# Layer 1's mixing modulation as row sums on VectorE inside layer 0's feed-forward loop, in place of TensorE products

## The chip, the core and the metric

The kernel runs on one core of a Trainium2 chip. The metric is the device time of one launch in microseconds (us), taken as the median of several runs. A core has TensorE (PE; its weight loads are shown apart as PEld), VectorE (DVE), ScalarE (ACT), GpSimd (POOL) and SyncE (SP). Each engine runs its own instructions in the order in which they stand in its queue and waits on semaphores for the others. Here SP does nothing but issue DMA transfers, also in the order of its queue.

## What is computed

Two layers of a diffusion backbone, for 128 context tokens and 256 latent tokens of width 1024, all in fp32. Each layer is modulated by vectors that come from a condition vector: `c_ctx` for the context, `c` for the latents. Cut to what the change touches:

```python
mod_ctx = (silu(c_ctx) @ w_mod[l] + b_mod[l])[None, :]      # w_mod[l]: 1024 x 6144
mod_lat = silu(c) @ w_mod[l] + b_mod[l]

def layer(x, mod, p, ...):
    sh1, sc1, g1, sh2, sc2, g2 = split(mod, 6)              # 1024 wide each
    h = layer_norm(x) * (1 + sc1) + sh1
    z = h @ p["w_in"] + p["b_in"]                           # q, k, v, conv, fourier, gates
    merged = ga * a_attn + gc * a_conv + gf * a_f           # attention, convolution, Fourier mixing
    x = layer_norm(ALPHA * x + g1 * (merged @ p["w_o"]), ...)
    h = layer_norm(x) * (1 + sc2) + sh2
    u = dwconv(h @ p["w_up"], ...)                          # 1024 -> 5632
    ug, uv = split(u, 2)
    x = layer_norm(ALPHA * x + g2 * ((silu(ug) * uv) @ p["w_down"]), ...)
```

The change concerns `sh1` and `sc1` of layer 1, for both condition vectors: 2 x 1024 sums of 1024 products for each of the two vectors. Layer 1 needs them when its first normalised activations are transposed, at the end of layer 0.

## The kernel before

**Arithmetic.** A matrix product is made of three TensorE products (`mm3`, L192): both operands are split into a high part of type fp32r and a low part that is the rest. For weights, `halves` (L169) does that: ScalarE copies a half of the loaded tile to `whi` (L177), VectorE subtracts it to get `wlo` (L178). There are five buffers for `whi`, five for `wlo` and three for the loaded 1 MB tiles `raw`, so both engines run some tiles ahead of TensorE and are let on as TensorE gives buffers back.

**Order.** The program is written in one order. When it is built, a scheduler places the instructions of each engine in a queue and sets the waits; tiles come from pools with a fixed number of buffers for each tag (`BUFS`, L79), and an instruction that needs a buffer waits for its last user. TensorE's results have two PSUM buffers `ps` and six `acc`. All input loads stand in SP's queue (`load`, L120).

**Modulation.** `setup` (L131) loads the two condition vectors as 16 x 128, takes silu of them (L146 to L148; the result is the tile `ch`), transposes it and keeps it as the stationary operand `cpad`. The modulation is cut into groups A (`sh1`, `sc1`), B (`sh2`, `sc2`) and G (the gates). Group A of layer 0 is made at the start (`mod_first`). All others run through `mod_stream` (L235): a step loads two row blocks of the weights as eight tiles of 256 KB, multiplies them by `cpad` (L215), and adds up in an `acc` buffer over four steps. After the fourth step of an A or B group, `mod_columns` (L276) copies the sums to SBUF (L280, VectorE), turns them into columns with four TensorE transposes (L284) and adds the bias into `modcol` (L292). In layer 0's mixing the stream has three groups, (0,G), (0,B) and (1,A), so twelve steps. `mixing` (L478) calls it once every two tiles of its three branches (L563 to L577). The four steps of (1,A) fall into the last branch.

**Around it.** The last branch makes, for each of eight output tiles, a gate (`ws_tile`, 24 products) and a projection (6 products). VectorE and GpSimd merge them (L531, L532), and the result is split (L535, L536) into `m_hl`. Then come the `w_o` products (`layer`, L814): the first three of the eight row blocks into six `acc` buffers, then the other five for one output part at a time (`tail`), so that closing the first token tile (`close`, L780) overlaps with the products of the next.

**The feed-forward loop** (L902) has 11 rounds. A round makes four tiles of 24 products (`up_tile`, L891) into the two `ps` buffers, each followed by ScalarE's L895 and VectorE's L896 and L898, after which the buffer is free again. VectorE's L914, L916 and L919 and ScalarE's L913 and L918 make the gated result. `down` adds 36 products into `acc`. A round splits six weight halves. The first round's four tiles are made ahead of the loop from unsplit operands (L869), while the three token tiles are closed one after another.

Of the kernel before, what the change touches and what calls it, by code (L numbers as in the profile page):

```python
# [10 lines left out]
F32 = mybir.dt.float32  # L11
F32R = mybir.dt.float32r
AF = mybir.ActivationFunctionType
ALU = mybir.AluOpType
AX = mybir.AxisListType

P = 128
D = 1024
# [59 lines left out]
class Net:  # L78
# [52 lines left out]
    def setup(self):  # L131
        nc, a = self.nc, self.a
        self.zeros = self.const("zeros", [P, P])
        nc.vector.memset(self.zeros, 0.0)
        self.busy(self.WARM)
        self.ident = self.const("ident", [P, P])
        make_identity(nc, self.ident)
        self.mhalf = self.const("mhalf", [P, 1])
        nc.gpsimd.memset(self.mhalf, -0.5)
        self.zero2 = self.const("zero2", [P, 2 * KD])  # L140
        nc.gpsimd.memset(self.zero2, 0.0)
        self.cpad = self.const("cpad", [P, KD, 32])
        nc.gpsimd.memset(self.cpad, 0.0)
        ct, ch = self.kk()[0:2 * KD, :], self.kk()[0:2 * KD, :]
        self.load(ct, a["c2"])
        nc.vector.tensor_scalar(ch, ct, 0.5, None, op0=ALU.mult)  # L146
        nc.scalar.activation(ct, ch, AF.Tanh)
        nc.vector.scalar_tensor_tensor(ch, ct, 1.0, ch, op0=ALU.add, op1=ALU.mult)  # L148
        pt = self.psum()
        nc.tensor.transpose(pt[:, 0:2 * KD], ch, self.ident[0:2 * KD, 0:2 * KD])  # L150
        nc.vector.tensor_copy(
            self.cpad[:, :, 0:2], pt[:, 0:2 * KD].rearrange("p (v k) -> p k v", v=2))
        self.gscr = self.dr.tile([DEPTH, 2, 2, D], F32, tag="gscr", name="gscr", bufs=1)
        self.xscr = self.dr.tile([3, P, D], F32, tag="xscr", name="xscr", bufs=1)

# [120 lines left out]
    def mod_columns(self, l, kind, ps, n, k0, tag):  # L276

        nc = self.nc
        row = self.s2()[:, 0:n]
        nc.vector.tensor_copy(row, ps[:, 0:n])  # L280
        pt = self.psum(tag)
        ns = n // P
        for q in range(ns):
            nc.tensor.transpose(pt[:, q * P:(q + 1) * P], row[:, q * P:(q + 1) * P], self.ident)  # L284
        for j in range(2):
            gi = j + (2 if kind == "B" else 0)
            ks = slice(k0, k0 + 2 * ns)
            bias = self.bmod[l][:, j + (3 if kind == "B" else 0), ks].rearrange("p (i q) -> p i q", q=ns)
            for v in range(2):
                part = pt[:, 0:n].rearrange("p (q j i r) -> p j r i q", q=ns, j=2, i=2)[:, j, v]  # L290
                dst = self.modcol[l][:, gi, v, ks].rearrange("p (i q) -> p i q", q=ns)
                nc.vector.tensor_tensor(dst, part, bias, op=ALU.add)  # L292

    def gate_bc(self, l, j):
        out = []
# [518 lines left out]
    def layer(self, l, first, hT, mods):  # L814
# [57 lines left out]
        for t in range(3):  # L872
            for q in range(2):
                self.split_hT(t, 4 * q, 4, h2f[t][q], h2, GAP)

        gT = {}
        off2 = (0, P, 2 * P + GAP)
        held = []
# [23 lines left out]
        for u in range(KF // 2):  # L902
            ws = []
            for v in range(2):
                if 2 * u + v * KF in pre:
                    ws.append([None, None])
                else:
                    ws.append(self.halves(self.col_halves(self.raw(a["w_u"][l, u, v]))))
            for h in range(2):
                i = 2 * u + h  # L910
                cg = up_tile(i, ws[0][h])
                th = self.g()
                nc.scalar.activation(th, cg, AF.Tanh)  # L913
                nc.vector.scalar_tensor_tensor(cg, th, 1.0, cg, op0=ALU.add, op1=ALU.mult)  # L914
                cv = up_tile(KF + i, ws[1][h])
                nc.vector.tensor_tensor(cg, cg, cv, op=ALU.mult)  # L916
                hi, lo = self.r(), self.r()
                nc.scalar.copy(hi, cg)  # L918
                nc.vector.tensor_tensor(lo, cg, f32(hi), op=ALU.subtract)  # L919
                gT[i] = (hi, lo)  # L920
            if u >= 1:
                down(u - 1)
        down(KF // 2 - 1)
# [47 lines left out]
    def run(self):  # L971
        self.setup()
        xhat = [self.s4() for _ in range(3)]
        for t in range(3):
            self.load(xhat[t], self.x_src(0, t))
        self.columns(0)
        for x in xhat:
            self.norm(x, x, D)
        mods = [[(0, "G"), (0, "B"), (1, "A")], [(1, "G"), (1, "B")]]
        first, hT = xhat, self.new_hT(0)  # L980
        for l in range(DEPTH):
            first, hT = self.layer(l, first, hT, mods[l])
# [11 lines left out]
def layout(i):  # L994
# [17 lines left out]
    def padded(*parts):  # L1012
# [9 lines left out]
        padded(rt(a["b_mod"]))], 2)  # L1022
    g = a["w_mod"].reshape(L, KD, P, 6, D)
    mod = np.stack([g[:, :, :, [0, 1]], g[:, :, :, [3, 4]], g[:, :, :, [2, 5]]], 1)
    kvf = cat([w_in[:, :, C_K:C_CONV], w_in[:, :, C_F:C_G]], 2)
    up = a["w_up"]
    out = {
# [5 lines left out]
        "b_g": np.stack([a["b_mod"][:, 2 * D:3 * D], a["b_mod"][:, 5 * D:6 * D]], 1),  # L1033
        "ln": np.stack([a["ln1_g"], a["ln1_b"], a["ln2_g"], a["ln2_b"]], 1),
        "w_mod0": mod[0, 0].reshape(2, 4, P, 2, 4, 256).transpose(4, 0, 2, 3, 1, 5),
        "w_mod": mod,
        "w_z": np.stack([rows(kvf), rows(w_in[:, :, C_Q:C_K])], 1),
        "w_cv": cols(w_in[:, :, C_CONV:C_F]), "w_g": cols(w_in[:, :, C_G:]),
        "w_f": rows(a["w_fnet"]), "w_c": rows(a["w_conv_o"]), "w_a": cols(a["w_attn_o"], 512),
# [21 lines left out]
```

## Time and profile before

| | us |
|---|---|
| median of 3 runs | 1173.68 (1172.41 to 1175.15) |
| the profiled execution, its own time | 1176.06 |
| span of its profile | 1174.3 |
| TensorE busy | 1149.9 (98% of the span) |
| VectorE busy | 753.3 (64%) |
| ScalarE busy | 523.1 (45%) |
| DMA queue of SP, mean share of 16 engines | 46.6% |

The profile is one execution. Its timelines give, for an engine, the start of an operation in us from the start of the span, its duration, its line and operation, the tiles written and read (buffer numbers left out), and in brackets how long the engine had been idle before it and what released it. The table of stretches gives in each row: the stretch, its length, the busy time of PE, PEld, DVE, ACT and POOL with their instruction counts, the clock that TensorE was granted as a share of full speed, the share of the DMA engines' time that was busy, and GB/s. The chain that ended last follows the work back from the last instruction to whatever released each step. TensorE's products overlap in time, so their spacing from start to start says more than their durations.

### The profile page before, as it was taken

Reading aid. Unit: us, or ns where it says so; the run is one execution under the profiler, and the core shown is the slowest. Engines: PE = TensorE matmul, PEld = TensorE weight load, DVE = VectorE, ACT = ScalarE, POOL = GpSimd, SP = SyncE. Lnnn points to the kernel's source line nnn. Section 1 sums busy time; section 2 is a strip of 40 time slices with the busy share of each in tenths; the row PEclk is TensorE's granted clock in tenths of the full one; section 3 lists DMA queues with packets and bytes.
Section 4 is the critical chain, followed back from the end, with each engine's and each line's share of the span. In section 5 each row is a group of like instructions: output and inputs, shape, how many; then the busy total and the mean of one; then the engine's idle time right before and its main releaser. Section 6 shows DMA issues by size and latency. Waiting matters only on the chain.

```text
span 1174.3 us, 16765 instructions
## 1 busy us (share of the span) xinstructions
PE 1149.9 (98%) x6637; PEld 1023.2 (87%) x6637; DVE 753.3 (64%) x1269; ACT 523.1 (45%) x875; POOL 77.4 (7%) x91
## 2 busy tenths in 40 slices
PE   8999999998999999999999999999999999999996
PEld 6788888887899999999966978889989999999995
DVE  5579965443776655566685699554567666655668
ACT  2456743232374443444454676433437444434440
POOL 1010001120100000000011000011211000000001
PEclk8999999998999999999999999999999999999998
DMA  9764568864273434343425545594335433333311
GB/s 374 274 209 138 178 218 290 301 232 165 72 251 108 144 108 144 108 145 108 143 82 189 180 157 201 198 334 144 134 108 216 143 108 124 128 129 123 129 51 54
DMA packets 49791, 194.90 MB, mean 166 GB/s; under 512 B 5760, under 2 KB 6800, under 8 KB 34608
## 3 DMA queue, kind: packets, MB, share of 16 engines
q1 hardware_dynamic: 49280, 193.04, 46.6%
q8 instruction: 52, 0.85, 0.3%
q10 hardware_dynamic: 432, 0.79, 0.2%
q14 instruction: 27, 0.22, 0.1%
HBM read 190.37 MB, written 3.44 MB: 165 GB/s over the span
## 4 chain that ended last, share of the span: by engine, by line
PE 86%; DVE 6%; DMA 3%; ACT 2%; POOL 1%; issue 1%; SPq 0%; POOLq 0%; DVEq 0%; ACTq 0%
PE ps L194 16%; PE ps L196 16%; PE ps L195 16%; PE acc L194 9%; PE acc L195 9%; PE acc L196 9%; PE acc L215 3%; PE acc L736 1%; PE acc L957 1%; DMA s<-w_z 1%; PE acc L724 1%; ACT whi L177 1%; DVE wlo L178 1%; PE ps L869 1%; POOL sm L345 1%
## 5 line engine op out<-in xcount | busy, mean ns | idle before, releaser
L178 DVE TENSOR_TENSOR wlo<-raw,whi 128x1024 fp32r<-128x1024 f32 x216 | 269.2, 1248 | 272.0 <-ACT whi L177 271.9
L194 PE MATMUL ps<-hT,whi 128*128 128x386 f32 (+1 forms) x1088 | 370.5, 341 | 1.5 <-ACT g L517 1.5
L196 PE MATMUL ps<-hT,wlo 128*128 128x386 f32 (+1 forms) x1088 | 368.7, 339 | 0.0
L195 PE MATMUL ps<-hT,whi 128*128 128x386 f32 (+1 forms) x1088 | 368.5, 339 | 0.0
L177 ACT CAST whi<-raw 128x1024 fp32r<-128x1024 f32 x216 | 225.7, 1048 | 307.6 <-PE ps L195 198.1
L194 PEld LDWEIGHTS ps<-hT,whi 128*128 128x128 f32 x1088 | 205.3, 189 | 15.3 <-ACT whi L177 5.9
L195 PEld LDWEIGHTS ps<-hT,whi 128*128 128x128 f32 x1088 | 205.2, 189 | 2.6 <-issue 1.7
L196 PEld LDWEIGHTS ps<-hT,wlo 128*128 128x128 f32 x1088 | 205.3, 189 | 0.3 <-issue 0.3
L195 PE MATMUL acc<-wlo,r 128*128 128x512 f32 x360 | 143.2, 398 | 0.0
L194 PE MATMUL acc<-whi,r 128*128 128x512 f32 x360 | 143.2, 398 | 0.0
L196 PE MATMUL acc<-whi,r 128*128 128x512 f32 x360 | 142.8, 397 | 0.0
L196 PEld LDWEIGHTS acc<-whi,r 128*128 128x128 f32 x360 | 68.2, 189 | 16.6 <-DVE r L919 0.5
L194 PEld LDWEIGHTS acc<-whi,r 128*128 128x128 f32 x360 | 68.3, 190 | 15.3
L195 PEld LDWEIGHTS acc<-wlo,r 128*128 128x128 f32 x360 | 68.2, 189 | 14.8
L754 DVE SCALAR_TENSOR_TENSOR cv<-upad,cst,cv 128x399 f32<-128x399 f32 x120 | 70.1, 627 | 0.1
L918 ACT CAST r<-g 128x386 fp32r<-128x386 f32 x44 | 22.7, 515 | 97.5 <-DVE g L916 97.5
L345 POOL TENSOR_TENSOR sm<-sm,mhalf 128x1 f32<-128x1 f32 x21 | 22.9, 1096 | 620.2 <-DVE sm L344 615.3
L895 ACT ACTIVATE g<-ps,cst 128x386 f32<-128x386 f32 x84 | 56.3, 671 | 0.0
L898 DVE SCALAR_TENSOR_TENSOR g<-ps,cst,g 128x385 f32<-128x385 f32 x84 | 52.1, 620 | 2.8
L896 DVE SCALAR_TENSOR_TENSOR g<-ps,cst,g 128x385 f32<-128x385 f32 x84 | 51.6, 615 | 0.3
L532 POOL TENSOR_TENSOR g<-g,g 128x384 f32<-128x384 f32 x32 | 35.8, 1118 | 188.0 <-DVE g L531 177.5
L913 ACT ACTIVATE g<-g 128x386 f32<-128x386 f32 x44 | 23.2, 528 | 51.9 <-DVE g L898 51.9
(182 smaller groups left out, 1322.4 us busy)
## 6 DMA issues: line engine op xcount, KB each, us to landing
raw<-w_u SPq DMA_DIRECT2D x44, 1024.0 KB, 4.8
s<-w_mod SPq DMA_DIRECT2D x160, 256.0 KB, 4.2
raw<-w_g SPq DMA_DIRECT2D x24, 1024.0 KB, 7.3
raw<-w_d SPq DMA_DIRECT2D x22, 1024.0 KB, 4.8
raw<-w_mod SPq DMA_DIRECT2D x8, 1024.0 KB, 10.9
raw<-w_o SPq DMA_DIRECT2D x8, 1024.0 KB, 5.5
s<-w_z SPq DMA_DIRECT2D x8, 512.0 KB, 9.0
raw<-w_cv SPq DMA_DIRECT2D x4, 1024.0 KB, 11.0
```

Source lines behind the costliest of these rows:

```text
L177: self.nc.scalar.copy(hi, raw)
L178: self.nc.vector.tensor_tensor(lo, raw, f32(hi), op=ALU.subtract)
L194: mm(ps, lh, rh, start=first, stop=False)
L195: mm(ps, lh, rl, start=False, stop=False)
L196: mm(ps, ll, rh, start=False, stop=last)
L215: self.nc.tensor.matmul(ps[32 * i:32 * i + 32, 0:n], self.cpad[:, k, :], src[k, i], start=ks[0] == 0 and k == ks[-1], stop=ks[-1] == KD - ...
L345: nc.gpsimd.tensor_tensor(mv[:, 3:4], mv[:, 2:3], self.mhalf, op=ALU.pow)
L532: nc.gpsimd.tensor_tensor(merged[m], merged[m], gt, op=ALU.add)
L754: nc.vector.scalar_tensor_tensor(c, u[:, i:i + CV_W], w, c, op0=ALU.mult, op1=ALU.add)
L895: nc.scalar.activation(c, ps, AF.Identity, bias=cols["ffn_b"][:, i:i + 1], scale=w[1])
L896: nc.vector.scalar_tensor_tensor(c[:, 1:NPAD], ps[:, 0:NPAD - 1], w[0], c[:, 1:NPAD], op0=ALU.mult, op1=ALU.add)
L898: nc.vector.scalar_tensor_tensor(c[:, 0:NPAD - 1], ps[:, 1:NPAD], w[2], c[:, 0:NPAD - 1], op0=ALU.mult, op1=ALU.add)
```

## The change

A new generator, `mod_rows`, takes the place of the group (1,A) in the stream. The weights of that group are laid out once more, transposed: 16 tiles of 128 output columns by 1024 inputs, 512 KB each, so that the two layouts move the same number of bytes. The silu vectors are written to a DRAM scratch `cscr` at the start, by a DMA on SP's queue. In layer 0's feed-forward loop each vector is loaded back, broadcast to 128 partitions. For each weight tile and each vector, one VectorE `scalar_tensor_tensor` multiplies 128 x 1024 elements and leaves the row sums in `accum_out`, 32 instructions in all; after each eight tiles two small additions put in the bias. The tiles are double-buffered. The generator is called once in every half round from round 2 on. Its tiles `cb`, `prod` and `w` take five of the eight `s4` buffers.

```diff
@@ setup
+        self.cscr = self.dr.tile([2, D], F32, tag="cscr", name="cscr", bufs=1)
+        nc.sync.dma_start(self.cscr.rearrange("v (k p) -> (v k) p", p=P), ch)
...
+    def mod_rows(self, l, kind):
+        nc, a = self.nc, self.a
+        cb = [self.bcast(self.cscr[v]) for v in range(2)]
+        prod = self.s4()
+        w = [self.s4() for _ in range(2)]
+        b0 = 3 if kind == "B" else 0
+        tiles = [(j, k) for j in range(2) for k in range(KD)]
+        sums = [self.sm(16) for _ in range(2)]
+
+        def fetch(n):
+            j, k = tiles[n]
+            self.load(w[n % 2], a["w_modr"][l - 1, self.MODS[kind], j, k])
+
+        fetch(0)
+        fetch(1)
+        yield
+        for n, (j, k) in enumerate(tiles):
+            for v in range(2):
+                nc.vector.scalar_tensor_tensor(prod, w[n % 2], 1.0, cb[v], op0=ALU.mult, op1=ALU.mult,
+                                               accum_out=sums[j][:, v * KD + k:v * KD + k + 1])
+            if n + 2 < len(tiles):
+                fetch(n + 2)
+            if k == KD - 1:
+                for v in range(2):
+                    nc.vector.tensor_tensor(self.modcol[l][:, j + (2 if kind == "B" else 0), v, :],
+                                            sums[j][:, v * KD:(v + 1) * KD], self.bmod[l][:, j + b0, :], op=ALU.add)
+            yield
...
@@ layer
+        rows = self.mod_rows(l + 1, "A") if l + 1 < DEPTH else iter(())
...
@@ the feed-forward loop, in each half round
+                if u >= 2:
+                    next(rows, None)
...
@@ run
-        mods = [[(0, "G"), (0, "B"), (1, "A")], [(1, "G"), (1, "B")]]
+        mods = [[(0, "G"), (0, "B")], [(1, "G"), (1, "B")]]
```

The scheduler's queues differ in three places that matter. Lines are those of the kernel that is shown; in the changed kernel they stand some lines lower (L177 and L178 at L179 and L180, L194 to L196 at L196 to L198, L284 at L286, L896 to L919 at L928 to L951).

TensorE's queue at the end of layer 0's merge, before: the last two of eight products of the fourth (1,A) step, the transposes of its sums, and the first `w_o` products.

```order
L215 MATMUL acc_2516<-s_2755,cpad 32x512
L215 MATMUL acc_2516<-s_2753,cpad 32x512
L284 MATMUL acc_2869<-ident,s_2867 128x128 x4
L194 MATMUL acc_2886<-whi_2894,r_2472 128x512
L195 MATMUL acc_2886<-wlo_2895,r_2472 128x512
L196 MATMUL acc_2886<-whi_2894,r_2473 128x512
```

The same place in the changed kernel: the last two products of the last branch, and then the `w_o` products at once.

```order
L197 MATMUL acc_2759<-r_2134,whi_2418 128x384
L198 MATMUL acc_2759<-r_2133,wlo_2419 128x384
L196 MATMUL acc_2780<-whi_2788,r_2458 128x512
L197 MATMUL acc_2780<-wlo_2789,r_2458 128x512
L198 MATMUL acc_2780<-whi_2788,r_2459 128x512
L196 MATMUL acc_2781<-whi_2788,r_2458 128x512
```

Of the 32 products and 4 transposes of (1,A), none is left in TensorE's queue; VectorE's copy L280 and the four additions L292 are gone from the same place.

SP's queue at the start, before: the loads of the tokens (`x_s`, `x_p`), of the parameter rows, and of the first weights.

```order
L121 DMA s_119<-x_s 128x1024
L121 DMA s_120<-x_p 128x1024
L121 DMA s_124<-par 128x512
L121 DMA raw_176<-w_mod 128x2048
L121 DMA raw_178<-w_mod 128x2048
L121 DMA s_221<-w_z 128x1024
```

The same place in the changed kernel.

```order
L121 DMA s_121<-x_s 128x1024
L121 DMA s_122<-x_p 128x1024
L154 DMA cscr<-kk_108 16x128
L121 DMA s_126<-par 128x512
L121 DMA raw_178<-w_mod 128x2048
L121 DMA raw_180<-w_mod 128x2048
L121 DMA s_223<-w_z 128x1024
```

The write of `cscr`, which waits for `ch` from L148, stands behind the token loads and ahead of the parameter rows and all weights.

VectorE's queue in the feed-forward loop, before: the start of round 2.

```order
L178 TENSOR_TENSOR wlo_3726<-raw_3723,whi_3725 128x1024
L178 TENSOR_TENSOR wlo_3730<-raw_3723,whi_3729 128x1024
L896 SCALAR_TENSOR_TENSOR g_3616<-ps_3591,cst_131,g_3616 128x385
L898 SCALAR_TENSOR_TENSOR g_3616<-ps_3591,cst_131,g_3616 128x385
L914 SCALAR_TENSOR_TENSOR g_3616<-g_3620,g_3616 128x386
L178 TENSOR_TENSOR wlo_3772<-raw_3769,whi_3771 128x1024
L896 SCALAR_TENSOR_TENSOR g_3648<-ps_3623,cst_131,g_3648 128x385
L898 SCALAR_TENSOR_TENSOR g_3648<-ps_3623,cst_131,g_3648 128x385
L916 TENSOR_TENSOR g_3616<-g_3616,g_3648 128x386
L919 TENSOR_TENSOR r_3654<-g_3616,r_3653 128x386
L896 SCALAR_TENSOR_TENSOR g_3682<-ps_3657,cst_131,g_3682 128x385
```

The same place in the changed kernel. `s_3555` is `prod`, `sm_3558` the sums, `s_3556` and `s_3557` the two weight buffers, `s_3551` and `s_3553` the two vectors.

```order
L180 TENSOR_TENSOR wlo_3638<-raw_3631,whi_3637 128x1024
L928 SCALAR_TENSOR_TENSOR g_3510<-ps_3485,cst_133,g_3510 128x385
L315 SCALAR_TENSOR_TENSOR s_3555,sm_3558<-s_3557,s_3551 128x1024
L930 SCALAR_TENSOR_TENSOR g_3510<-ps_3485,cst_133,g_3510 128x385
L315 SCALAR_TENSOR_TENSOR s_3555,sm_3558<-s_3557,s_3553 128x1024
L180 TENSOR_TENSOR wlo_3680<-raw_3677,whi_3679 128x1024
L946 SCALAR_TENSOR_TENSOR g_3510<-g_3514,g_3510 128x386
L928 SCALAR_TENSOR_TENSOR g_3542<-ps_3517,cst_133,g_3542 128x385
L315 SCALAR_TENSOR_TENSOR s_3555,sm_3558<-s_3556,s_3551 128x1024
L930 SCALAR_TENSOR_TENSOR g_3542<-ps_3517,cst_133,g_3542 128x385
L315 SCALAR_TENSOR_TENSOR s_3555,sm_3558<-s_3556,s_3553 128x1024
L948 TENSOR_TENSOR g_3510<-g_3510,g_3542 128x386
```

The sums L315 are not spread over the rounds as the code calls them. Four stand at the head of the loop (two between the last two splits L178 and the last two L386, one between the first L896 and L898, one behind), six in round 1, nine each in rounds 2 and 3, and four in the first half of round 4. On TensorE, two and then four of the products of `down` are drawn between the tiles of rounds 2 to 4. On SP, the first loads of `cscr` and of the new weights take the place that the loads of the closing gates and norm parameters have before.

## Rows read from the trace of the kernel before

**Rows 1.** the table of stretches, its columns as explained in the section above.
```profile
6.00:8.00 2.00, 2.00 (x20) 2.00 (x19) 1.92 (x6) 0.00 (x0) 0.55 (x1) 1.00 1.04 418
280.00:285.00 5.00, 5.00 (x15) 3.88 (x15) 0.00 (x0) 0.00 (x0) 0.00 (x0) 0.61 0.00 0
332.00:334.00 2.00, 1.62 (x15) 1.57 (x15) 1.47 (x2) 2.00 (x8) 0.00 (x0) 1.00 0.44 180
420.00:480.00 60.00, 60.00 (x319) 56.75 (x318) 36.82 (x49) 25.66 (x36) 0.00 (x0) 1.00 0.35 123
```

**Rows 2.** PE in time order (start, duration, operation), one modulation step.
```profile
234.35 0.34 PE L195 MATMUL acc<-r,whi 128*128 128x384 f32 x1
234.53 0.34 PE L196 MATMUL acc<-r,wlo 128*128 128x384 f32 x1
234.79 1.92 PE L215 MATMUL acc<-s,cpad 128*32 128x512 f32 x16
...
236.94 0.34 PE L195 MATMUL ps<-hT,whi 128*128 128x384 f32 x1
```

**Rows 3.** PE in order of time, the start of layer 0's `w_o` products.
```profile
272.25 0.34 PE L196 MATMUL acc<-r,wlo 128*128 128x384 f32 x1
...
277.96 1.11 PE L284 MATMUL acc<-ident,s 128*128 128x128 f32 x4 [3.52 <-DVE s L280]
...
283.96 0.40 PE L194 MATMUL acc<-whi,r 128*128 128x512 f32 x1
284.19 0.39 PE L195 MATMUL acc<-wlo,r 128*128 128x512 f32 x1
```

**Rows 4.** VectorE in order of time, the same stretch.
```profile
267.23 1.23 DVE L178 TENSOR_TENSOR wlo<-raw,whi 128x1024 fp32r<-128x1024 f32 x1 [3.33 <-ACT whi L177]
...
277.22 0.68 DVE L280 COPY s<-acc 128x512 f32<-128x512 f32 x1
```

**Rows 5.** SyncE's DMA queue in order of time, the start.
```profile
2.60 0.43 SPq L121 DMA_DIRECT2D s<-par  x1
```

**Rows 6.** VectorE in order of time, the start.
```profile
5.43 0.26 DVE L148 SCALAR_TENSOR_TENSOR kk<-kk,kk 16x128 f32<-16x128 f32 x1
```

**Rows 7.** the chain that ended last, the start: start, duration, what.
```profile
4.67 12.39 DMA s<-w_z
```

**Rows 8.** VectorE in order of time, layer 0's feed-forward loop.
```profile
371.50 0.61 DVE L896 SCALAR_TENSOR_TENSOR g<-ps,cst,g 128x385 f32<-128x385 f32 x1
...
396.81 0.61 DVE L896 SCALAR_TENSOR_TENSOR g<-ps,cst,g 128x385 f32<-128x385 f32 x1
...
404.73 0.62 DVE L898 SCALAR_TENSOR_TENSOR g<-ps,cst,g 128x385 f32<-128x385 f32 x1
405.27 1.22 DVE L178 TENSOR_TENSOR wlo<-raw,whi 128x1024 fp32r<-128x1024 f32 x1
406.40 0.56 DVE L914 SCALAR_TENSOR_TENSOR g<-g,g 128x386 f32<-128x386 f32 x1
```

**Rows 9.** VectorE in order of time, the way into that loop.
```profile
305.06 1.28 DVE L797 SCALAR_TENSOR_TENSOR s<-s,sm,s 128x1024 f32<-128x1024 f32 x1 [0.44 <-POOL sm L345]
...
306.38 0.15 DVE L356 TENSOR_SCALAR sm<-sm 128x1 f32<-128x1 f32 x1
...
331.11 2.36 DVE L178 TENSOR_TENSOR wlo<-raw,whi 128x1024 fp32r<-128x1024 f32 x2 [1.10 <-ACT whi L177]
335.35 1.29 DVE L386 TENSOR_TENSOR hT<-s,hT 128x512 fp32r<-128x512 f32 x2 [1.89 <-ACT hT L385]
```

**Rows 10.** SyncE's DMA queue in order of time, the same stretch.
```profile
324.62 2.07 SPq L121 DMA_DIRECT2D s<-ln  x2
```

**Rows 11.** PE in order of time, the first full product of the loop.
```profile
339.60 0.42 PE L194 MATMUL ps<-hT,whi 128*128 128x386 f32 x1
```

**Rows 12.** the DMA view: issues, count, KB each, median us to landing.
```profile
raw<-w_u SPq DMA_DIRECT2D x44, 1024.0 KB, 4.8
...
s<-ln SPq DMA_DIRECT2D x8, 512.0 KB, 9.4
```

More of the change, by code (lines that the diff above doesn't have):

```diff
@@ L1024, in layout @@
     mod = np.stack([g[:, :, :, [0, 1]], g[:, :, :, [3, 4]], g[:, :, :, [2, 5]]], 1)
+    modr = g[1:][:, :, :, [0, 1]].reshape(L - 1, D, 1, 2, KD, P).transpose(0, 2, 3, 4, 5, 1)
     kvf = cat([w_in[:, :, C_K:C_CONV], w_in[:, :, C_F:C_G]], 2)
@@ L1035, in layout @@
         "w_mod0": mod[0, 0].reshape(2, 4, P, 2, 4, 256).transpose(4, 0, 2, 3, 1, 5),
-        "w_mod": mod,
+        "w_mod": mod, "w_modr": modr,
         "w_z": np.stack([rows(kvf), rows(w_in[:, :, C_Q:C_K])], 1),
```

## The prediction

> **What bounds the kernel now.** I read the table of stretches first, then TensorE's timeline where the removed work stands, then the queues of VectorE and SP where the new work goes. In the feed-forward loop TensorE is busy for 60.00 of 60 us, VectorE for 36.82 [rows 1]. There VectorE has room, and an edit costs time only where it keeps TensorE waiting. In the merge of layer 0 the same holds, with one hole at its end: TensorE sits idle for 3.52 us until VectorE's copy L280 is done [rows 3], and right behind it the granted clock is 0.61, a mix of the 1.2 and the 2.4 GHz level [rows 1]. That hole is made by the group (1,A). The start is different: the chain runs through a `w_z` transfer of 12.39 us [rows 7], and the DMA engines are full (share 1.04, 418 GB/s) [rows 1].
>
> **Removed: three steps inside the merge.** A step's 16 records take 1.92 us. From the last product before them (234.53) to the second one after them (236.94) are 2.41 us; undisturbed it would be two spacings, and neighbours start 0.18 us apart (234.35, 234.53) [rows 2]. So a step costs 2.41 - 0.36 = 2.05 us, and three cost 6.2. All of it is on TensorE's path, because the neighbours are TensorE's own products without gaps.
>
> **Removed: the fourth step and what hangs on it.** The branch's last product starts at 272.25. Then come the products, the wait for the copy, the transposes, and the `w_o` products, of which the thirteenth starts at 283.96, the first at the full spacing of 0.23 us (283.96, 284.19) [rows 3]. In the new queue the first `w_o` product follows the branch's last one, so the thirteenth would start at 272.25 + 0.18 + 12 x 0.23 = 275.2. That is 8.8 us. It holds only if nothing else is late there. The third of the weight halves starts its split at 267.23, before the branch ends [rows 4]; the first three halves feed 54 products, or 12.4 us, and the later rows of `m_hl` are wanted only after these. The `acc` buffers are those of the last six projections, five of which VectorE has long read; the last is wanted 15 products (3.5 us) on. So I find nothing that is late next. With no idle time, I see no cause for the clock to fall there. Together the removals give 6.2 + 8.8 = **15.0 us**.
>
> **Added at the start.** SP is a queue: the write of `cscr` waits for L148, which ends at 5.43 + 0.26 = 5.69 [rows 6]. Behind it stand the parameter rows, issued at 2.60 before [rows 5], and all weights. They go out about 3.6 us later, with the write's own issue. That is the upper bound. But the DMA engines have the token loads to do meanwhile: 1.5 MB at 418 GB/s are 3.6 us, and they begin at about 2.5, so they last to about 6.2. The engines then stand idle from there until a transfer issued at about 6.2 begins to flow. `w_z` lands that much later and the rest follows, since TensorE's work hangs on it. The lower bound is 0.3. I take **1.0**, nearer to the rows on the full DMA engines than to the queue's own delay.
>
> **Added in the feed-forward loop: 32 sums.** The nearest row is L797, a `scalar_tensor_tensor` over 128 x 1024 fp32 with two SBUF operands and an accumulator: 1.28 us, and 1.32 to the next start (305.06, 306.38), which waits for the accumulator [rows 9]. Where the next one does not wait, starts come about 0.08 earlier than ends: L898 takes 0.62 but the next starts after 0.54, L178 1.22 and 1.13 [rows 8]. So a sum takes 1.20 to 1.32; I use 1.28.
>
> A round takes 396.81 - 371.50 = 25.31 us [rows 8]. VectorE's own work in it, by spacings: six splits at 1.13, eight of L896 and L898 at 0.54, six of the 0.56 us kind at 0.48 [rows 8], 14.0 us. By busy time it is 36.82 / 60 x 25.31 = 15.5 [rows 1]. Rounds 2 and 3 get nine sums: 14.0 + 11.5 = 25.5 us, which is 0.2 over the round; at the upper ends 15.5 + 11.9 = 27.4, 2.1 over. Rounds 1 and 4 have six and four and give time back. What may be lost before TensorE notices? A `ps` buffer is wanted again one tile later, 24 x 0.18 = 4.3 us. VectorE needs L896, one sum and L898 for it, 0.54 + 1.28 + 0.62 = 2.4, and ScalarE's step stands ahead of that. So something near 1 us of lateness is free, and the `down` products that are drawn between the tiles add to it. At my values the two dense rounds cost nothing, at the upper ends about 2 x 2.1 - 1 = 3.2.
>
> At the head of the loop there is less room. The two splits end at 331.11 + 2.36 = 333.47 [rows 9]. Two sums then end at 336.0, and the last two L386, which began at 335.35, move back by 0.7. With the third sum, the first L898 ends at about 339.8, and TensorE wants its buffer at 339.60 [rows 11]. The fourth delays the next buffers. I take **1.0** for the head, between 0 and four whole sums (5.1). The loads for these sums take the place that the norm rows have now; those are issued at 324.62 [rows 10], and by 332 to 334 the DMA share is down to 0.44 [rows 1], so they are in by 333.47.
>
> The Trainium skill speaks against this change in "Vector Engine (DVE) Microarchitecture Reference", section "Points that are easy to get wrong": an instruction of this scalar-tensor-tensor shape with two non-bf16 SBUF sources runs at half throughput, since no port is left for the accumulator. By it a sum would take about 2.4 us. L797 is such an instruction and takes 1.28 us; the row decides, and the rule's outcome is the third rival.
>
> **Sum.** 1176.06 - 15.0 + 1.0 + 1.0 = 1163.1 for an execution like the profiled one. That one is 2.4 us above the median of the runs, so I forecast **1160.7 us**.
>
> **Rivals.** *First: another wait fills the hole before `w_o`.* The order of the queues only says that L280's wait is gone; a late buffer, weight half or row of `m_hl` could hold TensorE for about as long and drop its clock again. For it: the merge's last links run through VectorE, GpSimd and ScalarE one after another. Against it: the split at 267.23 [rows 4]. Then only the four steps are gained, 8.2 us: 1173.7 - 8.2 + 2.0 = 1167.5.
>
> *Second: the sums wait for their loads, and it ends slower.* Two buffers hold the weights; a tile's load can go only when the second sum on its buffer is done, and SP has raw loads ahead of it at times. At 4.5 tiles in a round a tile comes every 5.6 us, its own two sums span about 3.9 with what stands between, so a load has about 2 x 5.6 - 3.9 = 7.3 us on average. A 1 MB weight load lands in 4.8 us; the norm rows, 512 KB each and broadcast, in 9.4 [rows 12]. The new loads are not broadcast, so I hold with 4.8. At 9.4 each of 14 loads is 2.1 late, 29 us of VectorE standing still, with the splits and the release of `ps` queued behind it; TensorE would lose some 27: 1187. From a landing time of about 8.3 us on the gain is gone.
>
> *Third: the sums take twice their time* (the rule above). Rounds 2 and 3 would need 14.0 + 9 x 2.4 = 35.6, 10.3 over each; round 1 28.4, 3.1 over; the head 4.5 more. 28 us lost: 1189. Break-even is at about 1.9 us a sum.
>
> **How the numbers follow.** Forecast 0.76; first rival 0.10; second 0.09, of which 0.05 end slower and 0.02 level; third 0.03; 0.02 for a start or a loop so much dearer that it ends level. The forecast's own range goes from 1158 (start 0.3, loop nothing, and a little for the spread of the runs) to 1166 (the start at 3.6 or the loop at 5). To leave out no more than two in ten it need reach the first rival, so 1157.5 to 1168.5. A difference under 0.2%, 2.3 us, is about what measuring this kernel can't tell from none. Faster 0.88, same 0.04, slower 0.08.
>
> **What would show it.** After the change TensorE's products run from the last projection into `w_o` with no L284 between and the clock stays at 1.00; if a wait stands there, the first rival is right and I am 7 us too low. The sums read 1.2 to 1.3 us; if 2.4, the third. VectorE's idle time ahead of L315 names a load or it doesn't: the second. At the start, the second `w_z` half should land about 1 us later than now; 3.6 would make the bound the truth. In rounds 2 and 3 TensorE should stay busy throughout, with the first wait of about 1 us at the head of the loop.

## The result and the profile after

| | before | after |
|---|---|---|
| median of 4 runs each, us | 1173.57 (1172.41 to 1175.15) | 1162.18 (1161.43 to 1163.45) |
| the profiled execution, its own time | 1176.06 | 1162.13 |
| span of its profile | 1174.3 | 1160.3 |
| TensorE busy | 1149.9 (98%) | 1139.3 (98%) |
| VectorE busy | 753.3 (64%) | 785.1 (68%) |

The changed kernel takes 0.9899 of the time (95% interval 0.9887 to 0.9910), 11.4 us less on the medians. The forecast was 1160.7, and "faster" was right; it is 1.5 us too low. The two profiled executions differ by 13.93 us, not by 11.4: the profiled execution of before was one of its longer ones. That gap leads to the error.

In the code of the changed kernel the lines are L282 for the copy L280, L286 for the transposes, L315 for the sums, L928 and L930 for L896 and L898.

**Where the work was removed.** TensorE in order of time, the end of layer 0's merge, after; it answers to [rows 3].

```profile
265.78 0.34 PE L198 MATMUL acc<-r,wlo 128*128 128x384 f32 x1
265.95 0.39 PE L196 MATMUL acc<-whi,r 128*128 128x512 f32 x1
...
268.74 0.40 PE L196 MATMUL acc<-whi,r 128*128 128x512 f32 x1
```

The first `w_o` product starts 0.17 us behind the last projection, with no wait. The branch's last product was at 272.25, so the inner steps and the small shift at the start gave 6.47. The thirteenth `w_o` product stood at 283.96, so 15.22 are gained by there.

**Where the work was added.** VectorE in order of time, the head of layer 0's feed-forward loop, after; it answers to [rows 9].

```profile
318.91 1.23 DVE L315 SCALAR_TENSOR_TENSOR s<-s,s 128x1024 f32<-128x1024 f32 x1 [0.65 <-DMA s<-w_modr]
320.06 0.08 DVE L315 DVE_READ_ACCUMULATOR s<-s,s 128x1 f32 x1
...
323.07 1.21 DVE L315 SCALAR_TENSOR_TENSOR s<-s,s 128x1024 f32<-128x1024 f32 x1
324.21 0.08 DVE L315 DVE_READ_ACCUMULATOR s<-s,s 128x1 f32 x1
324.21 0.61 DVE L930 SCALAR_TENSOR_TENSOR g<-ps,cst,g 128x385 f32<-128x385 f32 x1
```

TensorE's first full product of the loop, after; it answers to [rows 11].

```profile
324.97 0.42 PE L196 MATMUL ps<-hT,whi 128*128 128x386 f32 x1 [0.33 <-DVE g L930]
```

The wait for a load is 0.65 us, and TensorE's wait behind it 0.33. The sum at 323.07 holds VectorE until 324.21, that is 1.14 us.

The groups of instructions by line, VectorE, after: operation, tiles and shapes with their count, then busy time, mean ns of one, and the idle time ahead of them.

```profile
L315 DVE SCALAR_TENSOR_TENSOR s<-s,s 128x1024 f32<-128x1024 f32 x32 | 38.9, 1216 | 0.8 <-DMA s<-w_modr 0.7
L315 DVE DVE_READ_ACCUMULATOR s<-s,s 128x1 f32 x32 | 2.6, 81 | 0.0
```

The table of stretches, after; the columns are those of [rows 1].

```profile
6.00:8.00 2.00, 2.00 (x15) 2.00 (x15) 1.90 (x8) 0.00 (x0) 0.55 (x1) 1.00 0.89 279
265.00:270.00 5.00, 5.00 (x25) 4.23 (x24) 3.11 (x5) 2.66 (x4) 1.86 (x1) 1.00 0.35 102
369.00:395.00 26.00, 26.00 (x136) 24.15 (x135) 25.10 (x42) 11.10 (x15) 0.00 (x0) 1.00 0.60 209
420.00:480.00 60.00, 60.00 (x309) 55.49 (x308) 36.79 (x48) 25.19 (x34) 0.00 (x0) 1.00 0.42 148
```

From 265 to 270 the clock is 1.00 where the same work had 0.61 behind the hole [rows 1]. In a dense round (369 to 395) VectorE is busy for 25.10 of 26 us, and TensorE for all of them. At 6 to 8 the DMA engines' share is 0.89 where it was 1.04 [rows 1]: the first weights go out later.

The chain that ended last, after, at the start; it answers to [rows 5, 7].

```profile
5.53 0.33 SPq L154
5.90 0.42 SPq L121
...
7.79 9.84 DMA s<-w_z
```

The write of `cscr` is issued at 5.53 and the parameter rows at 5.90, 3.30 later than before. The `w_z` half lands at 17.63, where it landed at 17.06: 0.57 later.

### The profile page after: what moved, and what is told of

It reads as the page before. It is cut to its first block, busy times and chain, and to the rows that moved or that the text cites. A ratio compares the mean times of both kernels' runs of the same rounds, so it can differ in the third digit from the quotient of the medians.

```text
span 1160.3 us, 16670 instructions
## 1 busy us (share of the span) xinstructions
PE 1139.3 (98%) x6569; PEld 1019.4 (88%) x6569; DVE 785.1 (68%) x1332; ACT 522.9 (45%) x875; POOL 77.5 (7%) x91
## 4 chain that ended last, share of the span: by engine, by line
PE 84%; DVE 8%; ACT 2%; DMA 2%; POOL 1%; issue 1%; SPq 0%; POOLq 0%; DVEq 0%; ACTq 0%
PE ps L196 16%; PE ps L198 16%; PE ps L197 16%; PE acc L196 9%; PE acc L197 9%; PE acc L198 9%; PE acc L217 2%; PE acc L767 1%; DVE sm L372 1%; DVE wlo L180 1%; POOL sm L376 1%; DVE s L818 1%; DVE s L828 1%; PE acc L755 1%; ACT whi L179 1%
## 5 line engine op out<-in xcount | busy, mean ns | idle before, releaser
L180 DVE TENSOR_TENSOR wlo<-raw,whi 128x1024 fp32r<-128x1024 f32 x216 | 269.1, 1247 | 236.2 <-ACT whi L179 227.2
L196 PE MATMUL ps<-hT,whi 128*128 128x386 f32 (+1 forms) x1088 | 370.3, 340 | 1.8 <-ACT g L548 1.5
L198 PE MATMUL ps<-hT,wlo 128*128 128x386 f32 (+1 forms) x1088 | 368.7, 339 | 0.0
L179 ACT CAST whi<-raw 128x1024 fp32r<-128x1024 f32 x216 | 225.8, 1049 | 308.1 <-PE ps L197 211.4
L196 PEld LDWEIGHTS ps<-hT,whi 128*128 128x128 f32 x1088 | 205.2, 189 | 14.1 <-ACT whi L179 5.0
L198 PEld LDWEIGHTS ps<-hT,wlo 128*128 128x128 f32 x1088 | 205.3, 189 | 0.3 <-issue 0.3
L196 PE MATMUL acc<-whi,r 128*128 128x512 f32 x360 | 142.1, 395 | 0.0
L198 PE MATMUL acc<-whi,r 128*128 128x512 f32 x360 | 141.9, 394 | 0.0
L198 PEld LDWEIGHTS acc<-whi,r 128*128 128x128 f32 x360 | 67.6, 188 | 16.2 <-DVE r L951 0.5
L196 PEld LDWEIGHTS acc<-whi,r 128*128 128x128 f32 x360 | 67.6, 188 | 14.9
L930 DVE SCALAR_TENSOR_TENSOR g<-ps,cst,g 128x385 f32<-128x385 f32 x84 | 52.0, 619 | 2.3
L928 DVE SCALAR_TENSOR_TENSOR g<-ps,cst,g 128x385 f32<-128x385 f32 x84 | 51.6, 614 | 0.2
```

The source lines that it names most:

```text
L179: self.nc.scalar.copy(hi, raw)
L180: self.nc.vector.tensor_tensor(lo, raw, f32(hi), op=ALU.subtract)
L196: mm(ps, lh, rh, start=first, stop=False)
L198: mm(ps, ll, rh, start=False, stop=last)
L928: nc.vector.scalar_tensor_tensor(c[:, 1:NPAD], ps[:, 0:NPAD - 1], w[0], c[:, 1:NPAD], op0=ALU.mult, op1=ALU.add)
L930: nc.vector.scalar_tensor_tensor(c[:, 0:NPAD - 1], ps[:, 1:NPAD], w[2], c[:, 0:NPAD - 1], op0=ALU.mult, op1=ALU.add)
```

## The experiments

**How they are read.** The executions of one kernel differ by some us, and in the profiles of before two stretches make the difference: the start, and the place behind the hole, which is TensorE's idle time of 3.52 us ahead of L284. So I also read two landmarks in TensorE's timeline of each kernel: A, the start of the sixth group of 32 modulation products at the start (35.77 before), and Z, the start of the first full-width transposes of layer 1 (597.96 before). Z - A holds the hole and the loop, and leaves out the start. For after and for `no_group` (below) they are these lines.

```profile
35.51 1.08 PE L217 MATMUL ps<-raw,cpad 128*32 128x128 f32 x32
583.51 1.03 PE L401 MATMUL ps<-ident,s 128*128 128x128 f32 x8
```

```profile
35.23 1.08 PE L215 MATMUL ps<-raw,cpad 128*32 128x128 f32 x32
582.48 1.03 PE L372 MATMUL ps<-ident,s 128*128 128x128 f32 x8
```

| kernel | median, us | A | Z - A | span - Z |
|---|---|---|---|---|
| before | 1173.57 | 35.77 | 562.19 | 576.3 |
| b_again | one run, 1174.33 | 36.38 | 559.51 | 576.7 |
| b_third | one run, 1173.29 | 34.19 | 560.99 | 576.3 |
| fill_hole | 1172.41 | 35.82 | 559.53 | 576.4 |
| late_cols | 1168.70 | 33.95 | 556.03 | 576.9 |
| no_group | 1160.02 | 35.23 | 547.25 | 576.3 |
| write_only | 1175.06 | 35.83 | 561.00 | 576.6 |
| sums_beside | 1178.02 | 36.42 | 563.07 | 576.5 |
| after | 1162.18 | 35.51 | 548.00 | 576.8 |
| after_again | 1163.25 | 36.88 | 547.82 | 576.8 |
| write_act | 1160.69 | 34.50 | 547.88 | 576.4 |
| double_sums | 1162.68 | 36.50 | 548.03 | 576.8 |
| rows_both | 1152.39 | 35.97 | 547.58 | 567.2 |
| both_act | 1151.58 | 35.49 | 547.92 | 567.1 |

Medians were taken beside runs of before with medians of 1173.56 (`no_group`, `late_cols`, `fill_hole`), 1174.08 (`write_only`, `write_act`, `sums_beside`, `rows_both`), 1172.75 (`double_sums`) and 1173.86 (`both_act`, `after_again`). The landmarks are of one profile each. The expectations of `after_again` and `b_third` give A by the chain of waits, which draws it 0.07 later (35.84), so that Z - A of before is 562.12 there.

### The removal: the steps, the hole and the clock

`no_group` takes the group away and puts nothing in its place: `sh1` and `sc1` of layer 1 are set to 1.0 by GpSimd, so that part of the computation is left out.

```diff
@@ where modcol is made
+        if l == 1:
+            nc.gpsimd.memset(self.modcol[l][:, 0:2], 1.0)
@@ run
-        mods = [[(0, "G"), (0, "B"), (1, "A")], [(1, "G"), (1, "B")]]
+        mods = [[(0, "G"), (0, "B")], [(1, "G"), (1, "B")]]
```

> The kernel before without the four (1,A) steps, their copy and transposes, and with nothing in their place (sh1 and sc1 of layer 1 are set to 1.0, so that part of the computation is left out). My sum (3 x 2.05 for the inner steps, 8.8 for the fourth with its hole and the clock behind it): 15.0 us less than before in one profile, 1158.6 on the medians. If the clock behind the hole falls only in some executions of before, the medians differ by 15.0 - 2.5 = 12.5: 1161. If the removed steps were worth only their TensorE time, 4 x 2.05: 1165.4. With the changed kernel at 1162.2, what it adds costs 3.6, 1 or less than nothing by these three.

Measured: 1160.02 beside 1173.56, ratio 0.9881 (0.9864 to 0.9897), 13.5 us on the medians, between the first two expectations. Between the landmarks it is 562.19 - 547.25 = 14.94 against the first profile of before, and 559.51 - 547.25 = 12.26 against the second. So the removal is worth 15.0 in one execution of before and 12.3 in another. The value of the steps' TensorE time alone, 8.2, is excluded.

`late_cols` keeps the products. The sums of (1,A) are copied, and the transposes are made in the first round of the feed-forward loop.

```diff
@@ mod_stream, after the fourth step of (1,A)
-                    self.mod_columns(l, kind, ps, 512, 0, "acc")
+                    row = self.s2()
+                    self.nc.vector.tensor_copy(row, ps)
+                    self.held_row = row
@@ mod_columns, called without ps
+            row = self.held_row
@@ the feed-forward loop
+            if u == 0 and l == 0:
+                self.mod_columns(1, "A", None, 512, 0, "acc")
```

> The kernel before with all products of (1,A) kept; only what follows the fourth step is moved, the four transposes and the bias additions into the first round of the feed-forward loop. It takes the hole away and leaves the steps. If the hole and the clock behind it cost what I worked out, 8.8 - 2.05 = 6.7 us, the time is 1166.9. If the clock falls in some executions of before only, 4 to 5: 1169. If the first rival's mechanism was there to be met (another wait fills the hole as soon as the copy is gone), under 1: 1173.

Measured: 1168.70 beside 1173.56, ratio 0.9954 (0.9940 to 0.9967), 4.9 us, inside the second expectation. TensorE in order of time, `late_cols`:

```profile
270.71 1.92 PE L215 MATMUL acc<-s,cpad 128*32 128x512 f32 x16
272.56 0.50 PE L194 MATMUL acc<-whi,r 128*128 128x512 f32 x1
272.90 0.40 PE L195 MATMUL acc<-wlo,r 128*128 128x512 f32 x1
```

VectorE's copy in the same kernel:

```profile
275.44 0.68 DVE L259 COPY s<-acc 128x512 f32<-128x512 f32 x1
```

The `w_o` products follow the fourth step directly. VectorE's copy still starts only at 275.44, 2.88 us behind the first of them, and TensorE doesn't wait for it. So no other wait stood behind the one that was taken away. Z - A is 556.03: 3.48 less than in `b_again`, which is the idle time of 3.52 and no more, and 8.78 more than in `no_group`, which is four steps at 2.05, and 0.58 left for the transposes and what goes with them. The medians agree on that part: 1168.70 - 1160.02 = 8.7.

`b_again` and `b_third` are the kernel before, profiled again.

> The kernel before once more, for a second profile of it. If the clock behind the hole varies from execution to execution, the stretch 278 to 284 reads above 0.5 here and the span is some 2 us under 1174.3; if the 2.4 us by which the first profile stood above the median lie elsewhere (the start, layer 1), that place shows it.

> The kernel before, for a third profile. From the landmark at 35.84 (the fourth full modulation step of the start) to the one at 597.96 (the first full-width transposes of layer 1) before took 562.12 us with the clock at 0.50 behind the hole, and 559.44 with the clock at 1.00. If the clock behind the hole is all that varies between the two landmarks, this profile gives 559.4 plus 0.44 for each us that the clock stands at 0.50 after 278; if something else varies there, another number.

TensorE's transposes in `b_again`, and then the table of stretches there:

```profile
278.60 0.66 PE L284 MATMUL acc<-ident,s 128*128 128x128 f32 x4 [3.52 <-DVE s L280]
```

```profile
276.00:278.00 2.00, 0.00 (x0) 0.00 (x0) 0.62 (x2) 0.52 (x1) 0.79 (x1) 1.00 0.96 377
278.00:280.00 2.00, 1.40 (x8) 1.25 (x9) 0.99 (x6) 0.00 (x0) 0.00 (x0) 1.00 0.25 102
280.00:282.00 2.00, 2.00 (x10) 1.61 (x9) 0.00 (x0) 0.00 (x0) 0.00 (x0) 1.00 0.00 0
```

The same stretches in the first profile of before:

```profile
276.00:278.00 2.00, 0.04 (x1) 0.05 (x1) 1.22 (x3) 0.52 (x1) 0.15 (x1) 0.77 0.92 389
278.00:280.00 2.00, 2.00 (x7) 1.81 (x8) 0.39 (x4) 0.00 (x0) 0.00 (x0) 0.50 0.00 0
280.00:282.00 2.00, 2.00 (x6) 1.52 (x6) 0.00 (x0) 0.00 (x0) 0.00 (x0) 0.50 0.00 0
282.00:284.00 2.00, 2.00 (x7) 1.55 (x6) 0.00 (x0) 0.00 (x0) 0.00 (x0) 0.53 0.00 0
```

And in `b_third`, where the transposes start at 276.37:

```profile
276.00:278.00 2.00, 1.63 (x8) 1.38 (x9) 0.76 (x6) 0.00 (x0) 0.00 (x0) 0.77 0.09 37
278.00:280.00 2.00, 2.00 (x6) 1.62 (x5) 0.00 (x0) 0.00 (x0) 0.00 (x0) 0.50 0.00 0
280.00:282.00 2.00, 2.00 (x9) 1.56 (x9) 0.00 (x0) 0.00 (x0) 0.00 (x0) 0.88 0.00 0
```

The hole is the same in all three, 3.51 to 3.52 us. The clock behind it is not: at the 1.2 GHz level for about 5.9 us of work in the first, not at all in the second, for about 3.4 us in the third (0.92 + 2.00 + 0.48, from 0.77, 0.50 and 0.88). Z - A follows: 562.19, 559.51, and 560.99, where 559.5 + 0.44 x 3.4 = 561.0 (the first two profiles give 2.68 / 5.9 = 0.45 us lost for each us at 0.50). `write_only`, below, keeps the hole too; its clock is down for about 3.5 us there, and its Z - A is 561.00. So the clock behind the hole is what varies between the landmarks. `b_again` shows the other half too: with the clock up its start was slow (A at 36.38), and its whole time, 1174.33, is near the median. Here the first expectation, a span some 2 us under 1174.3, was right with 1172.6.

`fill_hole` leaves the wait and gives TensorE work in it.

```diff
@@ mod_columns, behind the copy
+        if (l, kind) == (1, "A"):
+            self.busy(16)
```

> The kernel before with 16 products of zeros between the fourth (1,A) step and the transposes, 16 x 0.18 = 2.9 us of TensorE work inside the hole of 3.52. The wait stays, the engine is not idle. If idle time there is what drops the clock, the clock stays at 1.00 from 278 to 284 and the time falls by the slow products' surplus, some 6 us at half clock = about 3 less: 1170.6. If the clock falls for another reason, 1173.6.

Measured: 1172.41 beside 1173.56, ratio 0.9984 (0.9976 to 0.9993). TensorE in order of time, and the stretches:

```profile
274.42 3.84 PE L129 MATMUL ps<-zeros 128*128 128x128 f32 x32
278.10 0.60 PE L286 MATMUL acc<-ident,s 128*128 128x128 f32 x4
```

```profile
278.00:280.00 2.00, 2.00 (x14) 1.73 (x13) 0.47 (x6) 0.00 (x0) 0.00 (x0) 1.00 0.00 0
280.00:282.00 2.00, 2.00 (x10) 1.63 (x9) 0.00 (x0) 0.00 (x0) 0.00 (x0) 1.00 0.04 8
```

The 16 products are recorded as 32 and fill the whole hole, with no idle time left. The useful work starts no earlier than before (278.10 and 277.96), and the clock stays at 1.00. Z - A is that of `b_again`, 559.53. One profile says little here, since in `b_again` the clock stayed up behind the open hole; what counts is all executions. The mean granted clock is 0.995 to 0.998 in the 12 of `fill_hole` and 0.991 to 0.997 in the 17 of before beside them, and the gain is 1.2 us on the medians (0.8 to 2.8 by the interval of the ratio). That it is less than 3 fits a clock that falls in some executions of before, and for part of the time in others.

### What the change adds

`write_only` is the kernel before with the write of `cscr`; `write_act` is the changed kernel with that write on ScalarE's DMA queue.

```diff
@@ write_only, in setup
+        self.cscr = self.dr.tile([2, D], F32, tag="cscr", name="cscr", bufs=1)
+        nc.sync.dma_start(self.cscr.rearrange("v (k p) -> (v k) p", p=P), ch)
@@ write_act, in setup
-        nc.sync.dma_start(self.cscr.rearrange("v (k p) -> (v k) p", p=P), ch)
+        nc.scalar.dma_start(self.cscr.rearrange("v (k p) -> (v k) p", p=P), ch)
```

> The kernel before plus the write of cscr on SP's queue and nothing else. By my sum it costs 1.0 us (1174.6), by the shift of the second w_z half in the two traces 0.57 (1174.2), by the queue's own delay 3.6 (1177.2); nothing if the clock's fall at the start takes it up (1173.6).

> The changed kernel with the write of cscr issued from ScalarE's DMA queue, so that SP's queue waits for nothing. par and the weights go out 3 us earlier than in the changed kernel. If the queue's wait costs what the traces show, 0.57 less: 1161.6; if 1.0, 1161.2; if the DMA engines hide all of it, 1162.2.

Measured: `write_only` 1175.06 beside 1174.08, ratio 1.0009 (1.0000 to 1.0018), about 1.0 us dearer, with an interval that begins at nothing. `write_act` 1160.69, ratio 0.9883 (0.9869 to 0.9897), 1.5 us under the changed kernel's median and below all three expectations; the intervals of the two ratios overlap. The stretch from 6 to 8 in `write_only`, and the same in `write_act`:

```profile
6.00:8.00 2.00, 2.00 (x20) 2.00 (x20) 1.95 (x5) 0.00 (x0) 0.46 (x1) 1.00 0.71 229
```

```profile
6.00:8.00 2.00, 2.00 (x21) 2.00 (x20) 1.93 (x6) 0.00 (x0) 0.55 (x1) 1.00 1.08 436
```

With the write on SP's queue the DMA engines run short of work for that moment: in the six profiles with it their share from 6 to 8 is 0.65 to 0.89, in the eight without it 1.01 to 1.08. The landmark A shows what that costs. In the eight it is at 33.95 to 36.38, 35.17 on average; in the six at 35.51 to 36.88, 36.19 on average: 1.0 us. The one pair of before and after says -0.26, since the start of before was a late one.

The clock could be a rival here, for it falls at the start too, and not for the same time in each profile. Here are `b_again` and then `late_cols`, which is the same kernel up to there:

```profile
22.00:24.00 2.00, 2.00 (x33) 1.39 (x32) 0.43 (x1) 0.50 (x2) 0.00 (x0) 0.50 1.05 432
```

```profile
22.00:24.00 2.00, 2.00 (x13) 1.58 (x9) 0.00 (x0) 0.81 (x1) 0.00 (x0) 1.00 1.06 436
```

Between 14 and 26 it is down for about 3.4 us in ten of the fourteen profiles, and for longer in `before`, `sums_beside`, `b_again` and `after_again`. Among the ten alone A is 34.86 on average without the write (six) and 35.95 with it (four), 1.1 us. So the difference doesn't come from the clock.

`sums_beside` is the changed kernel with the four steps, copy and transposes put back; the sums are done and dropped.

```diff
-        mods = [[(0, "G"), (0, "B")], [(1, "G"), (1, "B")]]
+        mods = [[(0, "G"), (0, "B"), (1, "A")], [(1, "G"), (1, "B")]]
@@ mod_rows
-                    nc.vector.tensor_tensor(self.modcol[l][:, j + (2 if kind == "B" else 0), v, :],
+                    nc.vector.tensor_tensor(self.sm(KD),
```

> The changed kernel with the four (1,A) steps, copy and transposes put back; the 32 sums are done all the same and their result is dropped. It is the kernel before plus all that the change adds. By my sum 2.0 us over before (1175.6); by the traces 0.57 at the start, 0.6 at the head of the loop and 0.1 in the rounds, 1.3 (1174.9); if the sums held TensorE in the dense rounds, 3 to 5 over (1177 to 1179).

Measured: 1178.02 beside 1174.08, ratio 1.0031 (1.0021 to 1.0041), 3.9 us. That lies in the third expectation by its number and not by its cause: between the landmarks the profile takes only 0.88 more than the first one of before, so TensorE isn't held in the rounds. The hole and the clock behind it in `sums_beside`:

```profile
278.59 1.12 PE L286 MATMUL acc<-ident,s 128*128 128x128 f32 x4 [3.51 <-DVE s L282]
280.00:282.00 2.00, 2.00 (x6) 1.59 (x5) 0.13 (x2) 0.00 (x0) 0.00 (x0) 0.50 0.00 0
282.00:284.00 2.00, 2.00 (x6) 1.54 (x5) 0.00 (x0) 0.00 (x0) 0.00 (x0) 0.50 0.00 0
```

The clock is down for about as long as in the first profile of before (0.50 and 0.53 in these stretches). But that profile (1176.06) is 2.0 us above the median beside which `sums_beside` is measured, and this one (1178.17) is at its own median. So the 3.9 us are 0.9 between the landmarks, 1.0 at the start, 0.3 outside the profile's span (the time is 2.1 us longer than the span in all 11 executions, 1.8 in the 21 of before beside them), and 1.7 that remain. A clock that is down longer in a middle execution of this kernel than in one of before would account for them, and the mean granted clock fits that (median 0.992, and 0.994 in the 21 of before). Why it should be down longer here, and what stands outside the span, stays open. In the changed kernel itself, where there is no hole, the sums cost 547.90 - 547.25 = 0.65 us (`after`, `after_again` and `write_act` against `no_group`).

`double_sums` does each sum twice.

```diff
-            for v in range(2):
+            for v in (0, 0, 1, 1):
                 nc.vector.scalar_tensor_tensor(prod, w[n % 2], 1.0, cb[v], op0=ALU.mult, op1=ALU.mult,
```

> The changed kernel with every sum done twice, 64 in all, each weight tile used four times, so that half the loads feed the same VectorE work. It makes a sum cost about 2.3 us for its tile, as the third rival said of one sum. By that rival's working, 28 us lost: 1190. If VectorE's queue simply takes the sums further down, into rounds 4 to 8, at the measured spacing of 1.14 us, there is room for 32 x 1.14 = 36.5 us in eleven rounds with some 9 us free in each: under 2 us lost, 1164.

Measured: 1162.68 beside 1172.75, ratio 0.9907 (0.9890 to 0.9923); Z - A is 548.03, as in the changed kernel. The table of stretches, `double_sums`, six rounds of the loop:

```profile
350.00:500.00 150.00, 150.00 (x784) 140.34 (x783) 146.42 (x229) 61.93 (x84) 0.00 (x0) 1.00 0.52 176
```

VectorE is busy for 146.42 of 150 us, 98%, and TensorE for all of them. The 32 added sums, 36 us of VectorE's time, cost 0.1 us between the landmarks, which is within the differences of the changed kernel's own profiles: the queue takes them further down, to 505, into rounds that had room. No 25 us hold more than ten of them, and in the changed kernel nine. So this run shows that nine sums in each of many rounds are free; it doesn't show what a round with nine sums of 2.4 us would cost, and the third rival's 28 us stay untested.

### Two versions that go further

`rows_both` does (1,B) the same way, in the same loop; `both_act` also moves the write of `cscr` to ScalarE's queue.

```diff
-        tiles = [(j, k) for j in range(2) for k in range(KD)]
+        tiles = [(g, j, k) for g in range(2) for j in range(2) for k in range(KD)]
...
-        mods = [[(0, "G"), (0, "B")], [(1, "G"), (1, "B")]]
+        mods = [[(0, "G"), (0, "B")], [(1, "G")]]
```

> The changed kernel with group (1,B) done in the same way, 64 sums in all, so that layer 1's stream has four steps and one copy with transposes less. If a step is worth 2.05 us on TensorE and VectorE has room for 32 more sums: 8.2 less, 1154.0. If the sums, now in seven to eight dense rounds, hold TensorE for 0.5 to 1 us a round, 1158 to 1162. If VectorE is over its room in every round, 1162 to 1175.

> Groups (1,A) and (1,B) both as row sums, and the write of cscr on ScalarE's DMA queue. If the start's cost of the write on SP's queue is real (1.0 to 1.5 us in the two runs so far), 1152.4 - 1.2 = 1151.2; if those differences were the spread of the start, 1152.4.

Measured: 1152.39 (ratio 0.9813, 0.9799 to 0.9826) and 1151.58 (0.9807, 0.9794 to 0.9821), some 10 us under the changed kernel. The first is below its lowest expectation, the second between its two, and the intervals overlap. The gain lies in layer 1 alone: span - Z falls from 576.8 to 567.2, 9.6 us. Of that, 8.8 is what four steps and their transposes were worth in layer 0, and 0.39 a wait of TensorE for their copy, which stands in the changed kernel's profile and not here; 0.4 isn't placed. Z - A stays at 547.6 to 547.9 with 64 sums in the loop.

`after_again` is the changed kernel once more.

> The changed kernel once more, beside the kernel above on one chip and with more executions of before than its first four. By the traces: before with the clock at half behind the hole 14.9 less (562.12 - 547.18 from one landmark to the next), 12.3 less with the clock at full, plus 0.7 for the sums and 1.0 for the write, so 10.6 to 13.2 less than before by how often the clock falls there; the middle, 11.9, gives 1161.8. If the write costs nothing, 1160.8.

Measured: 1163.25 beside 1173.86, ratio 0.9907 (0.9893 to 0.9920), 10.6 us: the lower end of the expected band. Its profile is of an execution at the median, with the latest A of all (36.88) and a clock at the start that is down for longer than in `after`.

## Why the prediction held, and where it was off

**The removal, 15.0.** Right for the execution it was worked out from: 14.94. By parts: steps and transposes 8.78 (6.2 + 2.05 and the transposes), idle time 3.48, clock 2.68.

**Nothing late next.** Right, by the mechanism too. The first rival would have shown in `late_cols` and in the timeline after; both run on without a wait, and the clock stays at 1.00.

**The start, 1.0.** Right on average (1.0 over 14 profiles, 1.0 in `write_only`, whose interval goes from nothing to 2.1), though the sign to look for, a `w_z` half that lands 1 us later, read 0.57 in one pair and says little: A lies anywhere from 33.95 to 36.38 without the write, so one pair of executions can't tell a shift of 1 us. The mechanism is the one named, engines that run dry for a moment at 6 to 8 us. The bound of 3.6 is far off.

**The loop's head, 1.0, and the dense rounds, nothing.** 0.65 together, of which 0.33 is the wait that was forecast, TensorE's for L930 (L898 before) at its first full product; where the rest lies isn't shown. That the first loads are in when VectorE is ready was wrong: the first sum waits 0.65 us for its own. The duration 1.28 was too high: 1.22, and the next operation starts 1.14 behind the sum's start. L797 [rows 9] has a per-partition operand and mean 1.28; L178's spacing of 1.13 [rows 8] was the better row.

**The second rival**, sums that wait for loads: 0.65 us, once. The new loads land in 4.2 us in the median.

**The third rival**, sums of twice the time by the rule in the Trainium skill's "Vector Engine (DVE) Microarchitecture Reference", section "Points that are easy to get wrong". A sum with two fp32 sources in SBUF and an accumulator takes 1216 ns for 128 x 1024. The subtraction of the same width, which has no accumulator, takes 1247. The rule doesn't hold for this instruction here.

**The step that failed: "That one is 2.4 us above the median of the runs, so I forecast 1160.7".** The sum gave 1163.1 for an execution like the profiled one. I then took off the profiled execution's surplus over the median as if all of it would stay. But part of it lay behind the hole, where this execution lost 2.68 us to the clock, and the change takes that place away. Over the executions of before the loss there is smaller: `no_group` gains 14.94 between the landmarks on the profiled one and 13.5 on the medians, and `fill_hole` 1.2 on the medians. So some 1.4 us were counted as a gain of the change and again as an offset. For a median execution the sum ought to have been 1173.6 - 13.5 + 2.0 = 1162.1, or 1161.7 with the additions as measured (1.0 and 0.65). Measured were 1162.18 and 1163.25. The rest of the surplus, about 1 us, lies in good part at the start (A at 35.77, 35.17 on average), and there an offset is right. That the clock falls behind the hole in every execution was an assumption from one profile; the prediction held it for a property of the kernel.

## What to carry to other kernels

Before a profile's time is scaled to the median, find the place in it that makes it slower than the median; if the change removes that place, the offset goes with it. Work for an engine with a third of its time free could here be put into its queue until it was 98% busy, with the results that the bounding engine waits for early enough in that queue. A small DMA with a wait, put into the queue of the loads, made that queue 3.3 us late and the kernel about 1.0, since the DMA engines ran dry only for a moment; on another queue it cost nothing that could be seen.

## What the runs showed of the hardware

- An idle time of TensorE of 3.52 us was followed by a granted clock of 0.50 for some 6 us, for some 3.4 us, or by no fall at all, in executions of one and the same program. Which it is isn't decided by anything that these profiles show.
- With TensorE kept at work on products of zeros in that time, the mean granted clock of the 12 runs was 0.995 to 0.998 and their times spread by 3.0 us, where the 17 of before beside them had 0.991 to 0.997 and 5.2 us.
- The accumulator's read, an instruction of its own of 81 ns, ran at the end of the sum's 1216 ns: the next operation started 1.14 us behind the sum's start.
